# Loading the first four row tiles of x in two column halves, one on each hardware DMA queue

## The chip, the cores and the metric

The kernel runs on one core of a Trainium2 chip. The metric is the device time of one execution in microseconds (us), and lower is better. Most executions of one kernel lie within 0.3% of each other.

## The reference

```python
# x (16, 512, 768), w1 (768, 3072), b1 (3072), w2 (3072, 768), all float32
y = np.matmul(x, w1) + b1
y = np.maximum(y, 0)
return np.matmul(y, w2).astype(np.float32)
```

Seen as one matrix, x has 8192 rows of 768 numbers. One row is 3072 bytes.

## The kernel before

The kernel multiplies in fp16 and uses a scheme that needs fewer block products than the plain one. TensorE is the bound for nearly the whole run. What matters here is its opening, the first 20 us.

The first 512 rows of x are fetched as four row tiles of 128 rows, in fp32, on the two hardware queues, which SyncE (`nc.sync`) and ScalarE (`nc.scalar`) issue: tiles 0 and 2 on the first, 1 and 3 on the second. Each partition of a tile takes one whole row.

```python
def load_x_first(self):
    self.first_rows = []
    for s in range(4):
        o = self.o_pool.tile([P, 2, self.NH], FP32, name="o")     # NH = 384
        o = o.rearrange("p a n -> p (a n)")
        (self.nc.sync, self.nc.scalar)[s % 2].dma_start(
            out=o, in_=self.xf[s * P:(s + 1) * P, :])
        self.first_rows.append(o)

def bias(self):                                                    # cut
    nc.scalar.dma_start(out=self.b1_rows, in_=self.b1.rearrange("(t p) -> t p", p=P))
```

The weights w1 come in strips, each of two transfers that GpSimd issues on its software queue and that turn fp32 into fp16 on the way. The next 512 rows of x (tile `xn`) take the same way.

```python
def load_strip(self, w, c, t):                                     # cut
    for half in range(2):
        self.nc.gpsimd.dma_start(out=w[:, 2 * half:2 * half + 2]..., in_=w1r[:, :, h0:h0 + P])

def run(self):                                                     # cut: the opening
    self.load_x_first()
    self.bias()
    self.load_w1(0)
    self.constants()              # GpSimd and VectorE: identity, ones, bounds
    self.load_w1(1)
    self.load_w1(2)
    self.load_x(0, (1,), 2)       # xn, in two parts
    self.load_w1(3)
    ...                           # w2 and more
    self.warm()                   # 8 matmuls of ones (x16 instructions in the trace)
    self.transpose_x_first(0)
```

TensorE first runs some matmuls of ones while it waits for x, then transposes the four tiles, six blocks of 128 x 128 each. VectorE copies the first three blocks out of PSUM, ScalarE the other three:

```python
def transpose_x_first(self, half, which=range(4)):
    for s in which:
        rows = self.raw[1][:, s, :] if half else self.first_rows[s]
        for a in range(2):
            ...
            for k in range(3):
                nc.tensor.transpose(ps[:, k, :],
                                    rows[:, (3 * a + k) * P:(3 * a + k + 1) * P], ident)
            o = self.x[:, 2 * half + a, :, s * P:(s + 1) * P]
            if a:
                nc.scalar.copy(out=o, in_=ps)
            else:
                nc.vector.tensor_copy(out=o, in_=ps)
```

Only when all four are done do the first products with w1 begin (line 563 of the kernel, in parts of 256 columns, then line 544 in full width). A few groups later the transposes of `xn` follow.

## Time and profile before

| what | before |
|---|---|
| median of three runs | 874.22 us (874.20 to 874.57) |
| span of the profiled run | 872.9 us |
| TensorE busy | 864.6 us |
| row tiles 0 to 3 of x landed, on the last engine | 5.18, 5.40, 7.01, 7.31 us |
| first packet of the software queue | 6.15 us |
| first product with w1 begins | 8.42 us |
| two parts of xn landed | 16.13, 18.08 us |

The landings are the times at which the last of the 16 DMA engines had added to the transfer's semaphore. How to read the rest: TensorE is idle for 8 us in 873, and nearly all of that lies at the two ends. The views of this kernel that the argument rests on stand in the prediction below. One view more will be needed, the timeline of TensorE over the first 9 us (start, length, line and operation, count, and in brackets the idle time ahead of it with its releaser):

```profile
5.32 1.50 PE L493 MATMUL ps<-ident,o 128*128 128x128 f32 x12 [0.38 <-DMA o<-in_x_dram]
7.05 1.53 PE L493 MATMUL ps<-ident,o 128*128 128x128 f32 x12 [0.23 <-DMA o<-in_x_dram]
8.42 0.82 PE L563 MATMUL ps<-x,w1s 128*128 128x256 f16 x6
```

The transposes come in two bursts, two tiles each, since the four loads land in two pairs.

### The profile page before, as it was taken

What the parts mean: (1) busy time and instruction counts of PE and PEld (TensorE: products, weight loads), DVE (VectorE), ACT (ScalarE), POOL (GpSimd) and SP (SyncE); (2) the same over time, 40 slices, a digit from 0 to 9 for tenths busy, and PEclk for the clock granted to TensorE, in tenths of its full rate; (3) what the DMA queues carried; (4) which work ended last, traced back from release to release, by engine and by line L of the source; (5) the groups of instructions that cost most, each with busy time, mean ns of one, the idle gap of its engine ahead of it and who ended that gap; (6) DMA issues with size and microseconds to landing.
All of it is one profiled execution on the core that took longest, in us unless ns stands there. A gap on an engine that the chain in (4) does not pass through costs nothing.

```text
span 872.9 us, 12620 instructions
## 1 busy us (share of the span) xinstructions
PE 864.6 (99%) x4693; PEld 458.8 (53%) x4693; DVE 621.4 (71%) x1082; ACT 521.3 (60%) x789; POOL 198.5 (23%) x175
## 2 busy tenths in 40 slices
PE   9999999999999999999999999999999999999997
PEld 7454554545545454554545546455454555545454
DVE  3898767767686667866799776666866758666676
ACT  5765667866677766676355776766626345263450
POOL 6310240603305041040200402203031130401325
PEclk9999999999999999999999999999999999999999
DMA  9999598796979959549551836539174482736724
GB/s 205 199 230 263 111 275 209 133 266 129 292 160 188 272 79 279 127 175 346 219 186 55 129 97 169 95 130 141 56 143 74 145 127 108 111 54 161 111 73 146
DMA packets 122532, 141.24 MB, mean 162 GB/s; under 512 B 67276, under 2 KB 115940, under 8 KB 118628
## 3 DMA queue, kind: packets, MB, share of 16 engines
q0 software_dynamic: 48512, 43.26, 35.0%
q1 hardware_dynamic: 73216, 95.76, 33.8%
q10 hardware_dynamic: 740, 1.39, 0.4%
q8 instruction: 37, 0.61, 0.3%
q14 instruction: 27, 0.22, 0.1%
HBM read 75.31 MB, written 77.66 MB: 175 GB/s over the span
## 4 chain that ended last, share of the span: by engine, by line
PE 97%; DMA 1%; POOL 1%; issue 0%; DVE 0%; POOLq 0%
PE ps L705 48%; PE ps L606 47%; PE ps L544 2%; DMA xn<-in_x_dram 1%; POOL w1s L332 1%; PE ps L563 0%; PE ps L493 0%; DVE o L738 0%; POOL ident masks.py:199 0%; POOL ident L285 0%; POOL high L300 0%; POOL low L301 0%; POOL ident masks.py:197 0%; PE ps L788 0%; PE ps L798 0%
## 5 line engine op out<-in xcount | busy, mean ns | idle before, releaser
L705 PE MATMUL ps<-v,y 128*128 128x384 f16 x2560 | 423.8, 326 | 0.0
L606 PE MATMUL ps<-x,w1s 128*128 128x512 f16 x1890 | 415.9, 379 | 0.0
L705 PEld LDWEIGHTS <-y 128*128 128x128 f16 x2560 | 249.3, 98 | 171.9 <-ACT y L623 2.7
L606 PEld LDWEIGHTS <-w1s 128*128 128x128 f16 x1890 | 184.7, 98 | 218.2 <-issue 1.0
L526 DVE TENSOR_TENSOR y<-y 128x512 f16<-128x512 f16 x512 | 204.6, 426 | 31.5 <-ACT y L623 24.1
L614 ACT ACTIVATE s<-ps,b1y 128x512 f32<-128x512 f32 x210 | 142.1, 686 | 136.1 <-PE ps L606 55.6
L618 DVE CUSTOM_DVE_ANT_0 y<-ps,s 128x512 f16<-128x512 f32 x210 | 144.9, 690 | 102.6 <-PE ps L606 71.3
L744 ACT ACTIVATE s<-ps 128x768 f32<-128x768 f32 x94 | 76.0, 809 | 112.7 <-PE ps L705 91.3
L763 POOL DMA_DIRECT2D out_dram<-o x54 | 66.4, 1375 | 315.9 <-DVE o L750 315.9
L750 DVE TENSOR_TENSOR s<-ps,s 128x768 f32<-128x768 f32 x96 | 90.2, 953 | 13.5 <-ACT s L744 6.7
L623 ACT ACTIVATE y<-ps,b1y 128x512 f16<-128x512 f32 x90 | 61.8, 687 | 37.5 <-PE ps L606 37.5
L750 DVE TENSOR_TENSOR o<-s,ps 128x768 f32<-128x768 f32 x53 | 50.4, 952 | 46.8 <-PE ps L705 23.2
L750 DVE TENSOR_TENSOR o<-ps,s 128x768 f32<-128x768 f32 x55 | 51.4, 953 | 31.8 <-ACT s L744 30.7
L452 POOL TENSOR_TENSOR x<-x 128x3072 f16<-128x3072 f16 x7 | 42.1, 6018 | 55.2 <-DVE x L449 43.5
L332 POOL DMA_DIRECT2D x<-in_w_dram x12 | 10.1, 848 | 183.8 <-PE ps L606 121.6
L440 ACT ACTIVATE scrap<-xn 128x768 f16<-128x768 f16 x60 | 50.4, 840 | 1.2
L629 ACT ACTIVATE ps<-ps,b1y 128x512 f32<-128x512 f32 x60 | 39.5, 659 | 10.3 <-PE ps L606 7.6
L744 ACT ACTIVATE ps<-ps 128x768 f32<-128x768 f32 x32 | 25.4, 795 | 17.9 <-PE ps L705 17.9
L623 ACT ACTIVATE y<-ps 128x512 f16<-128x512 f32 x60 | 35.8, 597 | 0.2
L401 ACT ACTIVATE scrap<-scrap 128x1536 f16<-128x1536 f16 x24 | 35.5, 1479 | 0.4
L427 POOL DMA_DIRECT2D xn<-in_x_dram x16 | 12.1, 759 | 69.4 <-ACT scrap L440 68.3
L544 PE MATMUL ps<-x,w1s 128*128 128x512 f16 x114 | 24.9, 379 | 0.0
(74 smaller groups left out, 303.3 us busy)
## 6 DMA issues: line engine op xcount, KB each, us to landing
out_dram<-o SPq DMA_DIRECT2D x54, 384.0 KB, 5.5
out_dram<-o POOLq DMA_DIRECT2D x54, 384.0 KB, 6.0
xd<-x SPq DMA_DIRECT2D x8, 1536.0 KB, 5.6
x<-xd SPq DMA_DIRECT2D x8, 1536.0 KB, 8.2
xn<-in_x_dram POOLq DMA_DIRECT2D x14, 768.0 KB, 9.3
xd<-x SPq DMA_DIRECT2D x7, 1152.0 KB, 9.6
x<-xd SPq DMA_DIRECT2D x7, 1152.0 KB, 5.3
out_dram<-x SPq DMA_DIRECT2D x16, 384.0 KB, 7.0
```

Of the source, the lines that this page charges most:

```text
L440: self.nc.scalar.activation(out=self.junk(self.K), in_=rows, func=ACTF.Square, accum_out=self.stat[:, i:i + 1])
L452: (self.nc.gpsimd if it > 1 else self.nc.vector).tensor_tensor(out=x[:, a21:self.XS2 + 1:self.XS2 - a21], in0=x[:, a21:self.XS1 + 1:self.X ...
L526: self.nc.vector.tensor_tensor(out=pair(*outs), in0=pair(*ins0), in1=pair(*ins1), op=ALU.add if sign > 0 else ALU.subtract)
L544: nc.tensor.matmul(ps, lhsT=w[:, ws[i], k, :], rhs=x[:, xs[i], k, :], start=(i == 0 and k == 0), stop=(i == 1 and k == 2))
L606: nc.tensor.matmul(ps, lhsT=w[:, slot, k, :], rhs=x[:, xslot, k, :], start=(start and k == 0), stop=(k == 2), skip_group_check=True)
L614: nc.scalar.activation(out=kept(name), in_=ps, func=ACTF.Identity, bias=bias)
L618: nc.vector._custom_dve(TENSOR_ADD_SAT, out=self.y_of(self.TP * half + t, m), in0=self.two(ps), in1=self.two(kept(name)), s0=F_MAX, s1=0.0)
L623: nc.scalar.activation(out=self.y_of(self.TP * half + t, m), in_=self.two(ps), func=ACTF.Relu, **kw)
L705: nc.tensor.matmul(self.ps[:, 2 * q + j, 0:NH], lhsT=self.y[:, U_OF[p], m0:m0 + P], rhs=self.v[:, V_OF[p], s, :], start=(start and s == 0) ...
L744: nc.scalar.activation(out=o, in_=ps, func=ACTF.Copy, scale=float(sign))
L750: nc.vector.tensor_tensor(out=o, in0=a, in1=b, op=ALU.add if sign == kept_sign else ALU.subtract)
L763: nc.gpsimd.dma_start(out=rows, in_=o, accum_op=ALU.add)
```

## The change

The intent: with both queues working on the same tile, tile 0 should be complete earlier than when each queue works on a tile of its own, and TensorE, which waits for x, could begin earlier. Each row of 3072 bytes is fetched as two pieces of 1536.

```diff
         for s in range(4):
             o = self.o_pool.tile([P, 2, self.NH], FP32, name="o")
-            o = o.rearrange("p a n -> p (a n)")
-            (self.nc.sync, self.nc.scalar)[s % 2].dma_start(
-                out=o, in_=self.xf[s * P:(s + 1) * P, :])
-            self.first_rows.append(o)
+            for a, queue in enumerate((self.nc.sync, self.nc.scalar)):
+                queue.dma_start(out=o[:, a], in_=self.xf[s * P:(s + 1) * P,
+                                                         a * self.NH:(a + 1) * self.NH])
+            self.first_rows.append(o.rearrange("p a n -> p (a n)"))
```

## The prediction

> **What bounds the kernel now.** I read the page first, for which engine is the bound and where its few idle microseconds lie; then TensorE's list of waits; then the chain of waits over the first 22 us, since the change touches nothing later; then the DMA queues in stretches, because the chain ends on a transfer there. The page: TensorE is busy 864.6 of 872.9 us, the mean granted clock is 0.999, and the slices show full digits everywhere.
>
> ```profile
> PE   9999999999999999999999999999999999999997
> ...
> PE 97%; DMA 1%; POOL 1%; issue 0%; DVE 0%; POOLq 0%
> ```
>
> The reader is to see that there is no slack on TensorE after the first slice: whatever the opening loses or wins moves the end by the same amount, and nothing but the opening can be won by a change of the first loads. TensorE's waits, all of the run, add up to 2.1 us (waits under about 0.1 us are not in the list):
>
> ```profile
> PE ps L415 <- DVE ones L294: 1.3, 1, 1.3
> PE ps L493 <- DMA o<-in_x_dram: 0.6, 2, 0.4
> PE ps L493 <- DMA xn<-in_x_dram: 0.2, 1, 0.2
> ```
>
> The second line is the one that the change aims at: the transposes of the first four row tiles (tile o) wait 0.6 us for x. It looks as if 0.6 us could be won. The chain of waits over the first 22 us (start, length, what) says otherwise:
>
> ```profile
> 8.01 8.11 DMA xn<-in_x_dram
> 16.13 0.05 issue
> 16.17 0.84 PE ps L493 x12
> 17.02 1.31 PE ps L563 x12
> 18.33 0.79 PE ps L493 x12
> ```
>
> The chain doesn't pass through tile o at all. It passes through xn, the second 512 rows of x, which GpSimd loads as fp16 in two parts: TensorE starts the transposes of the first part at 16.17, just after its landing at 16.13. The second part, issued at about 8.7 us, took 9.4 us to land, so it landed at about 18.1 us, and TensorE begins the transposes of it then, with hardly a gap (the modelled end of the matmul before is 18.32). So TensorE is pinned to a DMA landing twice, at 16.1 and at 18.1 us, and everything it does before can only be early for that.
>
> Why do these transfers take 8 to 9 us? The DMA queues, 0 to 6 us and then 7 to 18 us:
>
> ```profile
> q1 hardware_dynamic: 255, 0.73, 34.9%
> q10 hardware_dynamic: 216, 0.61, 27.6%
> ```
> ```profile
> q0 software_dynamic: 5668, 2.07, 158.0%
> q10 hardware_dynamic: 1, 0.00, 0.0%
> ```
>
> Until 6 us only the two hardware queues moved packets, although GpSimd issued its first w1 strips at 1.53 and 2.54 us. From 7 us on only the software queue moves, its packets taking 158% of the 16 engines' time (over 100%, since packets on one engine overlap). So the DMA engines are one serial resource from 2 us to beyond 18 us: x first (until about 6.8 us), then six w1 strips, then xn. The landing of xn is the end of that line, and what matters of x is **when its last byte has left the engines**, not when its first tile lands.
>
> **What the Trainium skill says.** All from the page "DMA: Bandwidth & Descriptors". (1) Section "Issuing engines are not separate DMA queues": DMAs of any issuing engine run on the same 16 DMA engines and interleave. The trace agrees as to the shared engines. (2) Section "Queues, rings and completion order": each engine goes round the queue rows that have work, at packet granularity. Here the trace does not look like it: no software packet in the first 6 us, though its issues are 3 us old. I can't tell from this trace whether the software descriptors were late or held back. (3) Section "Why small descriptors are slow (HBM only)": a fixed cost of about 3 cycles per packet at 32 bytes per cycle. For 3072 bytes this is 96+3 cycles, for twice 1536 bytes 2 x (48+3) = 102, so 3% more as an estimate from that page; the measured rates below show less. (4) Section "Why a DMA increments its semaphore by 16 and not by 1": use one semaphore per transfer in flight. This matters here, because the changed kernel has nine hardware transfers at the start where its semaphores are eight.
>
> **The change part by part.**
>
> Removed: four loads of 128 x 3072 bytes, two per queue. Added: eight of 128 x 1536 bytes, four per queue. Bytes the same, 1.57 MB; packets 512 become 1024.
>
> (a) Time on the DMA engines. Two stretches give the rate by packet size; the first holds 3072-byte reads of x (3 to 6 us), the second 1536-byte reads of earlier output (793 to 795.5 us):
>
> ```profile
> DMA packets 421, 1.20 MB, mean 398 GB/s; under 512 B 32, under 2 KB 32, under 8 KB 421
> ```
> ```profile
> DMA packets 682, 0.99 MB, mean 398 GB/s; under 512 B 35, under 2 KB 682, under 8 KB 682
> ```
>
> Without the semaphore packets (those under 512 B): 389 packets in 3 us over 16 engines are 123.4 ns per packet and engine; 647 in 2.5 us are 61.8 ns. So x needs 512/16 x 123.4 = 3.95 us before, and 1024/16 x 61.8 = 3.96 us after. The load of x ends where it did, the software queue starts where it did, and xn lands where it did: **0.0 us**, with 0.1 us (the page's 3%) as the size of what I may have missed.
>
> (b) The order of landings. Before, tiles 0 and 1 share the engines half and half and land at about 5.2 and 5.5 us (TensorE's first transpose starts at 5.32), tiles 2 and 3 at about 7.0 and 7.3. After, both queues work on tile 0, then on 1, 2, 3. Spread evenly over the same stretch these land at about 4.4, 5.3, 6.3 and 7.3 us. The first transpose can then start when the warm-up matmuls end (1.29 + 3.65 = 4.94 us), 0.4 us earlier. Tile 3, the last, lands as before; its six transposes (0.76 us, half of the 1.53 us for twelve) end at 8.1 to 8.2 instead of 8.58. So the wait of 0.6 us nearly goes, and the transposes end 0.4 us earlier.
>
> (c) What TensorE does with it. The next matmul (line 563) needs the first w1 strip: issued at 1.53 us, landed 6.8 us later, that is at 8.33; its weight load starts at 8.36. So that wait takes the place of the one removed, and about 0.0 to 0.1 us of the 0.4 is left. Were it all kept, there are still the landings of xn: TensorE had only 0.16 us to spare at 16.17.
>
> (d) The extra issues. Each costs its queue some 0.41 us (two took 0.91 us on ScalarE's, 0.87 on SyncE's), so ScalarE spends 0.8 us more. Besides, the built order of instructions shows a new wait: with eight semaphores for hardware transfers, the ninth, the bias load on ScalarE's queue, now waits for one half of tile 0 to land, about 4.4 us. ScalarE's activation table load stands behind it:
>
> ```profile
> 1.91 0.65 ACTq L309 DMA_DIRECT2D b_rows<-in_b_dram  x1
> 2.59 1.28 ACT L497 ACT_TABLE_LOAD   x1 [2.59 <-issue]
> ...
> 6.20 0.48 ACT L497 CAST x<-ps 128x384 f16<-128x384 f32 x1 [2.32 <-PE ps L493]
> ```
>
> So after: 4.4 + 0.65 + 1.28 = 6.3 us, against a first copy at 6.20 us before. The four copies of 0.48 us follow the transposes; the last, of tile 3, would end at about 8.7 (before 8.62 + 0.48 = 9.1). Even if the half landed at 5.2 us, four copies from 7.1 us end at 9.1, no later than before. The bias itself is transposed at 9.17 us; issued at 4.4 to 5.1 it stands in the queue behind the same halves of x as before, and 12 KB should land by 7.5 us. This **costs nothing**, if tile 0 isn't late.
>
> (e) All later hardware transfers move on by four of eight semaphores: a permutation, each still waits for the one eight before it.
>
> Sum on the path that sets the end: 0.0 (a), -0.1 to 0.0 (c), 0.0 (d). I put 874.3 us, the time of before and a tenth for the packets.
>
> **The rivals.** First, the wait for o is real and 0.4 us are won: 873.8. For it speaks the list of waits; against it the w1 strip at 8.33 and xn at 16.13 and 18.1. Second, twice the packets make the load of x longer, because the opening isn't in the steady state: between 2 and 4 us the engines were 84% busy and the rate was 267 GB/s, not 398. If half-sized packets fill the start worse, by up to 0.5 us, all the software line moves with it and TensorE too: 874.7. Third, the software queue gets more turns beside smaller packets: w1 earlier, tile 3 later, the sum of work the same and xn where it was: 874.2. Fourth, the bias or table load becomes the wait: only if tile 0 landed after about 6 us, against (b); then 0.3 to 0.5 us more. None reaches 1% of the time.
>
> **Range and chances.** The three runs before lie 0.37 us apart, as much as any effect here. With rivals of -0.4 to +0.5 us and this scatter, I take 873.7 to 875.0. A change of 2% would be 17.5 us, some thirty times the 0.6 us of wait; 98% for the same, 1% each side for an accident.
>
> **What would show it.** In the changed profile: first transpose at about 4.95 us and the wait on o under 0.3 us (b); a new short idle of TensorE or its weight load at about 8.2 to 8.4 us, put down to w1 or to issue (c); the table load at about 5.0 us (d); the software queue's first packets still after 6 us, and xn still landing at 16.1 and 18.1 us, within 0.2 (a). The prediction is wrong if the landings of xn move by more than 0.5 us, or if TensorE has a gap after 22 us that it hadn't.

## The result, and the profile after

| | before | after |
|---|---|---|
| median of six runs | 874.48 us (874.20 to 874.57) | 875.78 us (875.29 to 876.50) |
| span of the profiled run | 872.9 us | 873.9 us |

The ratio of after to before is 1.0016, with a 95% interval of 1.0003 to 1.0029. A ratio here is the mean time of one kernel's runs over that of the other's in the same rounds, so it is not quite the ratio of the medians. The result is correct and within 2%, as predicted, but it is 0.8 us above the top of the predicted range, and slower by more than the scatter. A repetition on another chip (the run e18 below) gave 875.98 against 874.43, ratio 1.0016 again.

The page of the changed kernel, its TensorE slices and the chain that ended last:

```profile
PE   8999999999999999999999999999999999999997
...
PE 98%; DMA 1%; issue 0%; SPq 0%; DVE 0%
```

The first slice has fallen from 9 to 8 and nothing else has changed: the time came from the opening. TensorE's wait for x (total us, number, longest):

```profile
PE ps L493 <- DMA o<-in_x_dram: 2.6, 2, 1.6
```

The wait for tile o, which the change aimed at, was 0.6 us and is now 2.6 us. The waits for xn have gone from the list. The chain of waits over the first 22 us (start, length, what) passes elsewhere than before:

```profile
2.37 7.23 DMA o<-in_x_dram
9.60 0.14 issue
9.74 0.85 PE ps L493 x6
```

It now runs through the half of tile 3 that was issued at 2.37 us and landed 7.2 us later, and no longer through xn. On TensorE's timeline:

```profile
4.52 1.57 PE L493 MATMUL ps<-ident,o 128*128 128x128 f32 x12
7.68 1.01 PE L493 MATMUL ps<-ident,o 128*128 128x128 f32 x6 [1.59 <-DMA o<-in_x_dram]
9.74 0.85 PE L493 MATMUL ps<-ident,o 128*128 128x128 f32 x6 [1.05 <-DMA o<-in_x_dram]
10.42 0.82 PE L563 MATMUL ps<-x,w1s 128*128 128x256 f16 x6
```

The reader is to see both faces of the change. The first two tiles did come earlier: their transposes start at 4.52 us instead of 5.32, with no wait at all. But tiles 2 and 3 were complete 1.1 and 2.5 us later (8.09 and 9.77 us), and as the products begin only after the fourth tile, the first of them starts at 10.42 us instead of 8.42.

The products need the first strip of w1 too. The weight load with which they begin, before and after:

```profile
8.36 0.59 PEld L563 LDWEIGHTS <-w1s 128*128 128x128 f16 x6
10.34 0.62 PEld L563 LDWEIGHTS <-w1s 128*128 128x128 f16 x6
```

The strip was complete at 8.31 us before, and at 10.29 after (10.18 in the repetition e18), both times just ahead of this line. So two late loads hold the first product at the same place: tile 3, whose last transposes run until 10.58, and the strip. With x on time alone it could not have begun before 10.3 us.

Here is how the 2.0 us travel to the end. The first full-width product (line 544 after the transposes of xn) starts at 22.85 instead of 21.00, 1.85 us later; the last group of 144 matmuls of line 705 on the chain at 843.55 instead of 841.97, 1.58 later; the span is 1.0 us longer in this pair of profiled runs, and 1.3 us in the medians. So the kernel gives back some 0.4 us of the 2.0 on the way. The last store is issued at 868.89 instead of 867.32, 1.57 later (1.47 in e18). What follows that store took 5.6 us before and 5.0 after, and anything from 4.1 to 5.8 us in the traces. This end scatters by more than the whole effect, so the last store is the better mark to compare two traces by.

Why did tile 3 land late? The DMA queues of the changed kernel over 0 to 6 us (packets, MB, share of the 16 engines' time) answer to those that the prediction shows for before:

```profile
q1 hardware_dynamic: 422, 0.58, 33.4%
q10 hardware_dynamic: 400, 0.55, 27.9%
q0 software_dynamic: 160, 0.04, 6.8%
```

Before, the two hardware queues had moved 0.73 + 0.61 = 1.34 MB by 6 us; now 0.58 + 0.55 = 1.13 MB, and the software queue is there already. Over 6 to 9.5 us, first before, then after:

```profile
q0 software_dynamic: 1998, 0.50, 145.3%
q10 hardware_dynamic: 108, 0.18, 14.3%
```
```profile
q0 software_dynamic: 1192, 0.30, 87.3%
q10 hardware_dynamic: 205, 0.25, 24.2%
q1 hardware_dynamic: 154, 0.21, 21.6%
```

In the changed kernel x and the software queue share the engines for all this stretch. My own count of the records of single packets, by the microsecond of their start, shows it more finely: KB of x (with the 12 KB of the bias), then packets of w1.

```text
us            2     3     4     5      6      7      8      9
before  KB  150   372   387   408    231      0      0      0
        w1    0     0     0     0    255    702     ..     ..
after   KB  216   336   342   207    160    165    112      8
        w1    0     0     0   160    278    180    415    611
```

Two things differ. From 3 to 5 us, with x alone on the engines in both kernels, the changed one moves 678 KB where the other moves 759; but from 2 to 3 us it had moved more, so that by 5 us the two are nearly level, at 894 and 909 KB. And the first software packet comes at 5.13 us instead of 6.15, with 606 KB of x still to move instead of 153. From then on x gets 110 to 210 KB per us where it had 400. Its last packet ends at 9.26 instead of 6.88 us. In this pair, then, nearly all of the difference comes after the software queue's early start. The stretches from 4 to 5 and 5 to 6 us (window, then the busy share of PE, PEld, DVE, ACT and POOL, the granted clock, the share of the DMA engines and GB/s) show the same, before and after:

```profile
4.00:5.00 1.00, 0.94 (x6) 0.75 (x4) 0.00 (x0) 0.00 (x0) 0.96 (x10) 1.00 1.03 396
5.00:6.00 1.00, 0.68 (x7) 0.71 (x7) 0.13 (x1) 0.00 (x0) 1.00 (x2) 1.00 1.03 418
```
```profile
4.00:5.00 1.00, 1.00 (x11) 1.00 (x10) 0.00 (x0) 0.14 (x1) 0.96 (x10) 1.00 0.97 350
5.00:6.00 1.00, 1.00 (x10) 0.73 (x7) 0.76 (x2) 1.00 (x1) 1.00 (x2) 1.00 1.21 253
```

From 396 and 418 GB/s to 350 and 253. Note that the DMA share is hardly lower, and in the second stretch higher: a share counts how long packets were under way, not how much they carried.

### The profile page after: what moved, and what is told of

Read it like the earlier page. It is cut to its first block, busy times and chain, and to the rows that moved or that the text cites. A ratio compares the mean times of both kernels' runs of the same rounds, so it can differ in the third digit from the quotient of the medians.

```text
span 873.9 us, 12627 instructions
## 1 busy us (share of the span) xinstructions
PE 864.3 (99%) x4693; PEld 459.2 (53%) x4693; DVE 621.5 (71%) x1082; ACT 521.1 (60%) x789; POOL 198.5 (23%) x175
## 4 chain that ended last, share of the span: by engine, by line
PE 98%; DMA 1%; issue 0%; SPq 0%; DVE 0%
PE ps L705 47%; PE ps L606 47%; PE ps L544 3%; DMA o<-in_x_dram 1%; PE ps L563 1%; PE ps L493 0%; SPq L478 0%; DVE o L738 0%; PE ps L315 0%; PE ps L788 0%; PE ps L798 0%; DVE o L750 0%
## 5 line engine op out<-in xcount | busy, mean ns | idle before, releaser
L623 ACT ACTIVATE y<-ps,b1y 128x512 f16<-128x512 f32 x90 | 61.8, 687 | 37.5 <-PE ps L606 37.5
L332 POOL DMA_DIRECT2D x<-in_w_dram x12 | 10.1, 848 | 184.3 <-PE ps L705 63.2
L629 ACT ACTIVATE ps<-ps,b1y 128x512 f32<-128x512 f32 x60 | 39.5, 659 | 10.3 <-PE ps L606 7.6
```

The lines of the kernel that those rows point to most:

```text
L623: nc.scalar.activation(out=self.y_of(self.TP * half + t, m), in_=self.two(ps), func=ACTF.Relu, **kw)
```

## The experiments

My theory after this comparison had two parts: pieces of 1536 bytes use the engines worse while x is alone on them, and the software queue then gets in while much of x is outstanding and takes turns with it. The rivals are named in the expectations, at some places by a letter: **W**, it is the bias load's wait for a half of tile 0, or the number of transfers against eight semaphores; the order of the halves over the queues; **P**, the engines handle only so many packets per time; **H**, it matters which tiles are split, not how many; **G**, each transfer needs some 0.5 us of preparation; **Q**, trouble comes after a fixed number of packets; **R**, it takes two queues with small packets. Eighteen runs were made, all with a correct result. In the text "x done" is the end of the landing of its last piece, and "the first product" the start of line 563 on TensorE (its number shifts a little with the edit).

### Halves by rows (e1)

```diff
+            for a, queue in enumerate((self.nc.sync, self.nc.scalar)):
+                r = slice(a * 64, a * 64 + 64)
+                queue.dma_start(out=o[r], in_=self.xf[s * P:(s + 1) * P, :][r])
```

Eight transfers as in the change, but with whole rows of 3072 bytes, 64 partitions each.

> Each of the first four row tiles is split by rows (64 partitions on each hardware queue) instead of by k: eight transfers and nine hardware transfers with the bias as in the change, both queues on one tile, but packets of 3072 bytes, 512 in all, as before the change. Theory A (small packets: with packets of 1536 bytes the software queue gets in before x is through and takes engine time from it): the first software packet at 6 us or later, the last tile landed by 7.5 us, 874.2 to 874.8 us. Rival B (number of transfers, the ninth on eight semaphores, or both queues on one tile): software packets from about 5.1 us, last tile landed at 9 us or later, 875.3 to 876.5 us as in the change.

Measured: 879.18 us (877.84 to 880.51) against 874.50, ratio 1.0059 [1.0042, 1.0075]; x done at 10.77 us, the first product at 11.99, the first software packet at 4.50 with 987 KB of x left. This is worse than the change. A packet of 3072 bytes took 155 ns in the median here, and 204 between 4 and 5 us, where it takes 121 ns in the kernel before. So the run is confounded: a transfer to 64 partitions is another thing than one to 128, and it can't tell how the number of transfers acts. It shows only that large packets alone don't make eight transfers harmless.

### Both halves on the tile's own queue (e2)

```diff
+            queue = (self.nc.sync, self.nc.scalar)[s % 2]
+            for a in range(2):
+                queue.dma_start(out=o[:, a], in_=...)     # as in the change
```

> The halves of k are kept, but both halves of a tile go on the tile's own queue as before the change (tiles 0 and 2 SyncE, 1 and 3 ScalarE). Same packets, same number of transfers per queue as in the change; only the order over the queues is the old one. Theory A (small packets): software packets from about 5.1 us, the last half landed at 9 us or later, 875.3 to 876.5 us. Rival C (both queues on one tile at a time): as the kernel before, last half landed by 7.5 us, 874.2 to 874.8 us.

Measured: 875.95 us (875.02 to 878.33), ratio 1.0013 [0.9996, 1.0030]; x done at 9.88, the first product at 11.55, the first software packet at 5.55 with 451 KB left. x is as late as in the change although tiles 0 and 1 are again loaded side by side. The order of the halves over the queues is not the cause of that. (The time alone would not show a loss, as the interval includes 1; and the trace is that of the slowest of the four runs, 878.33 us, with the clock at half from 10.4 to 13.7 us.)

### The software queue kept away from x (e3, e5)

```diff
-        self.load_w1(0)
         self.constants()
+        gate = self.const.tile([P, 2], FP32, name="gate")
+        for s in range(4):
+            self.nc.gpsimd.tensor_copy(out=gate, in_=self.first_rows[s][:, 0:self.K:self.NH])
+        self.load_w1(0)
```

GpSimd reads two columns of each tile before it issues w1, so x has the engines to itself. e3 is this on top of the change, e5 on top of the kernel before.

> The change, with the software queue kept empty until x has landed: GpSimd makes the constants first, then reads two columns of each of the four tiles, and only then issues the first w1 strip. Theory A (contention with the software queue): x alone lands by 7.4 us, as the prediction had it, in the order 4.4, 5.3, 6.3, 7.3. Rival D (two queues of half-sized packets are not supplied fast enough, whatever else runs): the last half lands at 8 us or later even so. In both the software line starts later than in the change, at about 9.5 us instead of 5.1, and the time is longer, about 877.5 to 878.5 us.

> The same gate on the kernel before the change: the pair of e3. x lands at 7.0 to 7.4 us as without the gate. Theory A: time within 0.3 us of e3 (877.5 to 878.5 us), since without contention the split costs nothing. Rival D: e3 is longer than this by 0.7 us or more.

Measured: e3 880.36 us, ratio 1.0064 [1.0047, 1.0081]; e5 879.90, ratio 1.0061 [1.0044, 1.0077]. Both are slow, as w1 comes late, and some 2 us slower than I had expected: after TensorE's long wait of 3 to 4 us its clock stayed at half for a while. The stretches tell the two apart. The stretches of e5 from 5 to 7 us, then of e3 (same columns as above):

```profile
5.00:6.00 1.00, 0.55 (x4) 0.50 (x4) 0.00 (x0) 0.00 (x0) 0.37 (x2) 1.00 1.02 415
6.00:7.00 1.00, 1.00 (x6) 1.00 (x6) 0.56 (x1) 0.00 (x0) 0.00 (x0) 1.00 0.61 234
```
```profile
5.00:6.00 1.00, 1.00 (x6) 1.00 (x6) 0.18 (x1) 0.82 (x1) 0.27 (x2) 1.00 0.89 315
6.00:7.00 1.00, 1.00 (x7) 1.00 (x7) 0.38 (x1) 0.94 (x2) 0.01 (x1) 1.00 0.88 320
```

With nothing else on the engines, whole rows move at 415 GB/s until they are through at 6.80 us; the halves at some 320, and they are through at 8.02. This is the cleanest pair: the split by itself costs x **1.2 us** on otherwise empty engines. Each is one trace, but five gated looks below agree in sign: from first packet to last, x took 4.79 us in e5, 6.00 in e3, and 5.1 to 6.6 in e11, e14, e17, e20 and e22, all with smaller packets than e5.

What the software queue adds is less certain. In the changed kernel x is through at 9.26 us (8.82 in e18), 1.2 (0.8) us after e3, where whole rows lose 0.1 by it (6.88 - 6.80). But the pair of e10 and e14 below, with packets of the same size, is through at 8.60 us with the software queue and at 8.64 without. So the cost of small packets alone is shown. That x moves more slowly once the software queue is in is shown too, by the KB above; how much later x ends for it, these runs don't settle, and the two costs can't simply be added.

### Small packets without more transfers (e10)

```diff
-            o = self.o_pool.tile([P, 2, self.NH], FP32, name="o")
-            o = o.rearrange("p a n -> p (a n)")
+            o = self.s.rearrange("p b n -> p (b n)")[:, s * 784:(s + 1) * 784]
+            o = o.rearrange("p (a n) -> p a n", a=2)[:, :, 0:self.NH]
             (self.nc.sync, self.nc.scalar)[s % 2].dma_start(
-                out=o, in_=self.xf[s * P:(s + 1) * P, :])
+                out=o, in_=self.xf[s * P:(s + 1) * P, :].rearrange("p (a n) -> p a n", a=2))
```

The four transfers of the kernel before, but into a buffer with a gap in the middle of each row, so that each is made of 256 packets of 1536 bytes. There are no more than eight transfers, so the bias load waits for nothing.

> The kernel before with its four transfers of x, but into a buffer with a gap between the halves of a row, so that each transfer consists of 256 packets of 1536 bytes: the change's packets (1024 in all) with the old number of transfers (four, no bias wait). Theory P (the packet count: more, smaller packets on the hardware queues let engines run out of hardware packets, and the software queue steps in early): first software packet at 5.0 to 5.7 us, last tile landed at 9 us or later, 875.0 to 876.5 us. Rival T (the number of transfers, each with its end on every engine): as the kernel before, first software packet at 6 us or later, last tile landed by 7.5 us, 874.2 to 874.8 us.

Measured: 876.25 us (875.88 to 877.02) against 874.29, ratio 1.0024 [1.0008, 1.0041]; x done at 8.95, the first product at 11.27, the first software packet at 5.40 with 597 KB left. x is nearly as late as in the changed kernel (9.77 us, and 9.25 in e18), without the change's transfers: it is **the packets**, and neither the number of transfers nor the bias load's wait. Two things are in the way of a finer reading. The first packet of x came at 2.42 us here, 0.4 later than before. And TensorE ran its transposes at half clock:

```profile
8.99 2.44 PE L496 MATMUL ps<-ident,s 128*128 128x128 f32 x12 [0.43 <-DMA s<-in_x_dram]
```

Twelve transposes took 1.53 us in the kernel before. So some 0.9 of the 2.5 us by which the last store is late in this trace (869.82 us) is the clock's, and not that of a late x.

### Which tiles are split (e6, e9, e4, e16, e19)

```diff
+            if s in (0,):          # e6; (0, 1) in e9, (1, 2, 3) in e4, (2, 3) in e16 and e19
+                ...                # two halves, as in the change
+            else:
+                ...                # whole, as before
```

> Only tile 0 is split over both queues, tiles 1 to 3 whole as before: five transfers of x and the bias, no wait on a semaphore before the bias. Both theories P and T: a quarter of the change, so most of x lands as before (last tile by 7.6 us) and the time is 874.3 to 874.9 us. If the dry engines come from any split at all: last tile at 9 us or later, 875.3 us or more. First transposes start at 4.95 us.

> Tiles 0 and 1 are split, 2 and 3 whole: half of the change (768 packets, six transfers of x). P and T: between, first software packet at 5.3 to 6.2 us, last tile landed at 7.3 to 8.5 us, 874.4 to 875.3 us.

> Tiles 1 to 3 are split, tile 0 is whole: seven transfers of x, so the bias is the eighth and does not wait for a landing; the activation table is loaded at about 3 us again. Rival W (the new wait of the bias and of the table load matters): 874.2 to 874.8 us as the kernel before. P and T: nearly the whole of the change, last tile landed at 8.5 us or later, 875.0 to 876.3 us.

> Tiles 2 and 3 are split, 0 and 1 whole: as many packets and transfers as e9, which split 0 and 1 and took 877.2 us, in the other order. Theory H (the feed must build up a lead with large packets before small ones come; a split at the start takes that lead away): last tile landed by 8.3 us, 874.2 to 875.0 us. Rival (only the number of small packets counts): as e9, last tile at 9 us or later, 875.6 to 878 us.

| run | split | us (n = 4) | ratio, 95% interval | first software packet (KB of x left) | x done | first product |
|---|---|---|---|---|---|---|
| e6 | 0 | 874.58 | 1.0005 [0.9989, 1.0022] | 5.92 (195) | 7.76 | 9.12 |
| e9 | 0, 1 | 877.21 | 1.0033 [1.0016, 1.0049] | 6.11 (420) | 9.18 | 11.25 |
| e4 | 1, 2, 3 | 874.63 | 1.0003 [0.9987, 1.0020] | 5.99 (313) | 8.45 | 9.27 |
| e16 | 2, 3 | 873.51 | 0.9993 [0.9976, 1.0009] | 6.00 (252) | 7.45 | 8.39 |

e4 alone looked like rival W: with three of four tiles split, but no wait of the bias load, the loss nearly vanishes. e9 and e10 contradict that, since they have no such wait either and lose. What tells them apart is where the small packets stand: e9 and e16 both split two tiles, so that they have the same number of transfers and packets, and x is done 1.7 us apart. The stretch from 4 to 5 us of e9 and of e16:

```profile
4.00:5.00 1.00, 1.00 (x7) 1.00 (x6) 0.00 (x0) 0.36 (x1) 0.95 (x10) 1.00 0.81 267
```
```profile
4.00:5.00 1.00, 0.75 (x6) 0.56 (x4) 0.00 (x0) 0.35 (x1) 0.96 (x10) 1.00 0.97 364
```

In e9 the engines are not full (0.81) from 4 us on, two microseconds before the first software packet. **Small packets hurt when they come first**, and cost next to nothing behind two tiles of whole rows (rival H was right). That the times of e4 and e6 lie within the scatter of before fits with their first product, 0.7 to 0.85 us later than 8.42, of which some is taken up again at xn.

I ran e16 a second time, with the change itself beside it, as its first result looked like a gain:

> e16 (tiles 2 and 3 split, 0 and 1 whole) beside e18 on one chip. Theory H (the first tiles must go whole, so that the feed gets ahead of the engines): last tile landed by 8 us, 873.2 to 874.6 us, less than e18 by 1 us or more. Rival (e16 was luck): 875 us or more.

> The changed kernel unaltered, for a second trace of its landings and as the partner of e19 on one chip. Software packets from 5.1 to 5.8 us, the last half of tile 3 landed at 9 to 10 us, 875.0 to 876.5 us.

Measured: e19 875.07 us (873.63 to 875.81), ratio 1.0012 [0.9995, 1.0028]; e18 875.98 (875.09 to 876.23), ratio 1.0016 [0.9999, 1.0033]. The landings repeat well: in e19 x is done at 7.59 and the first product starts at 8.40, in e18 at 9.25 and 10.22. The times of e16 and e19 don't agree with each other by 1.6 us, and their mean is that of before. In their two traces the last store is issued at the same 867.43 us, 0.11 after that of before; the difference lies behind it. So splitting tiles 2 and 3 is not shown to be faster or slower than before, and no version beats it.

### Why e9 lost more than the whole change (e15)

e9 splits half of what the change splits and loses 2.9 us against 1.3. TensorE's timeline of e9 around its gap:

```profile
9.03 2.43 PE L499 MATMUL ps<-ident,o 128*128 128x128 f32 x12 [2.09 <-DMA o<-in_x_dram]
11.25 1.49 PE L569 MATMUL ps<-x,w1s 128*128 128x256 f16 x6
```

After one wait of 2.09 us twelve transposes take 2.43 us instead of 1.5, and six products 1.49 instead of 0.82: TensorE ran at half clock, from 9.5 to 12.9 us (single transposes at 421 ns instead of 273). In the changed kernel the wait is broken into 1.59 and 1.05 us, and the clock stayed up. So I filled the gap:

```diff
+            for _ in range(8 if s == 2 and not half else 0):
+                nc.tensor.matmul(self.ps[:, 5, 0:P], lhsT=self.ones, rhs=self.ones, start=True,
+                                 stop=True)
```

> e9 (tiles 0 and 1 split) with eight matmuls of the warm-up kind between the transposes of tiles 1 and 2, where TensorE waited 2.1 us in e9 and then ran at half the clock (421 ns instead of 273 ns per matmul) until about 13 us. Theory K (the clock drop after the wait adds about 1.5 us): no half clock, 875.3 to 876.2 us, with the landings of e9. Rival (the late landing of x alone makes e9's time): 876.5 us or more, as e9.

```profile
9.32 1.53 PE L502 MATMUL ps<-ident,o 128*128 128x128 f32 x12 [0.33 <-DMA o<-in_x_dram]
10.69 0.82 PE L572 MATMUL ps<-x,w1s 128*128 128x256 f16 x6
```

Measured: 874.86 us (874.50 to 874.89) against 874.08, ratio 1.0009 [0.9992, 1.0025], somewhat better than expected. x is as late as in e9 (9.46 us), the clock stays full, and some 2 us of time have gone. The last store, 3.15 us later than before in e9, is 1.84 later here. The clock made most of e9's loss in time; it has no part in the change's, where the clock is 1.00 from 8 to 14 us. (e1, e2 and e23 have the same 3.4 us of half clock in their traces, so their times and first products hold more than a late x. "x done" does not depend on it.)

### Small packets alone on the engines: what kind of limit? (e11, e14, e17)

These and the next two are with the gate of e3, to see how x moves by itself. e11: as e10, with six pieces of 512 bytes per row. e14: e10 with the gate. e17: each tile in four quarters of columns, 16 transfers of 768-byte pieces on alternating queues.

```diff
+            for a in range(4):                                     # e17
+                cols = slice(a * 192, a * 192 + 192)
+                (self.nc.sync, self.nc.scalar)[a % 2].dma_start(
+                    out=o[:, cols], in_=self.xf[s * P:(s + 1) * P, cols])
```

> Measures the feed of the two hardware queues by packet count, with nothing else running: the kernel before, gated as e5, with each of the four transfers of x cut into 768 packets of 512 bytes (3072 in all). The software queue moved 512-byte reads at 22.9 ns per engine in the runs before (350 packets in 0.5 us), so the engines themselves could move 3072 of them in about 4.4 us. Theory P as a limit of feed (packets of the hardware queues come one every 4 ns or slower, whatever their size): x takes 12 us or more, from 2 to 14 us or later. Rival (the feed isn't limited by count, only unevenly shared): x is through by 7.5 us. The total is only a by-product: longer by some 2 us in the rival's case, by 8 us or more in P's.

> e10 (four transfers, 1024 packets of 1536 bytes) gated as e3 and e5, so x runs alone. In e3 (eight transfers of the same packets) its last packet ended at 8.02 us, in e5 (512 packets of 3072 bytes) at 6.80. Theory P (packet count): about 7.5 to 8.3 us here. Rival T (transfers): 6.8 to 7.1 us.

> What limits the feed: x in sixteen transfers of 128 packets of 768 bytes, gated, so that x runs alone. The first eight go out without a wait; each needs only some 0.26 us of the engines (8 packets of about 32 ns on each). Theory G (preparing a hardware transfer of 128 rows costs about 0.5 us, one transfer after another over both queues, so that with halves of k the feed just keeps pace with the engines and never gets ahead): the first landings of the first eight transfers come 0.45 to 0.6 us apart and the engines are busy 50 to 65% between 2.5 and 5 us. Rival (transfers are prepared faster; the dry engines have another cause): 0.25 to 0.35 us apart, busy 90% or more until the first eight are through.

Measured: e11 881.05 us, e14 880.22, e17 882.18 (against 874.1 to 874.4 of before). In e11 x needs from 2.43 to 8.20 us, 5.8 us for 3072 packets; in e14 from 2.42 to 8.64, 6.2 us for 1024 packets. Three times the packets in less time: a limit on packets per time (P) is out. In e17 the first six transfers land at 3.02, 3.20, 3.48, 3.76, 4.06 and 4.32 us on their first engine, 0.2 to 0.3 us apart, with the engines 88% busy or more; a preparation of 0.5 us for each (G) is out too. What e14 and e17 share is something else: from the third transfer (e14) or the fifth (e17) on, single engines fall behind. In e14 the third transfer was complete on the first engine at 5.91 and on the last at 8.04. From 7.4 to 8.6 us the engines were 7% busy, which is one of sixteen, with the last 20 packets of x. The records don't name a packet's engine; but 15 packets were in flight on average from 4.5 to 6.1 us, where it had been 17, so that an engine pausing there, which e20 takes for granted, is likely and not shown. In e17 the fifth transfer landed from 4.06 to 5.66.

In all kernels I looked for the same sign in single packets. I counted those that took over 250 ns and started after 4.5 us (a packet of 1536 bytes takes 65 ns, one of 3072 bytes 121):

```text
before 0   e5 0   e16 0   e19 0   e4 0   e6 4   after 10   e18 1   e2 2   e9 12   e15 11
e10 5   e3 2   e14 3   e22 6   e20 7   e11 0   e17 4   e23 7   e1 25
```

The five kernels whose first tile comes in whole rows of 128 partitions (before, e5, e16, e19, e4) have none; of the others all but e11 have some, up to 1151 ns long (after). But the count doesn't go with the loss: e6, without one, has four, more than e18 and e2. So this sign is not the whole of the matter.

### Later, or on one queue (e20, e22, e23)

```diff
+            self.nc.gpsimd.memset(o[:, 0, 0:1], 0.0)          # e20: e14, x issued later
+            self.nc.sync.dma_start(...)                       # e22: e14, all four on SyncE
+            self.nc.sync.dma_start(out=o[:, a], ...)          # e23: the change, all on SyncE
```

> e14 (x alone, four transfers of 256 packets of 1536 bytes) with x issued later, behind GpSimd's constants, by some 1.5 us. In e14 the third and fourth transfers landed unevenly (2.1 us between their first and last engine) because an engine paused from about 4.5 to 6.1 us. Theory Q (the pause comes after so many packets of the hardware queues): it moves with the issue, to 6 us or later, and the third and fourth transfers again spread by 1.5 us or more. Rival (something else at 4.3 to 6 us of the clock disturbs an engine): the pause stays at 4.5 to 6 us, in the first two transfers, and the last two spread by 1 us or less.

> e14 with all four transfers on SyncE's queue. Theory R (two queues taking turns make engines run dry, since the packets of the one are prepared behind those of the other): with one queue no pause, landings spread by 0.8 us or less, x through by 7.3 us. Rival Q (so many small packets, however queued): spread of 1.5 us or more in the last transfers, x through at 8 us or later.

> The change with all eight halves on SyncE's queue (ScalarE's has only the bias), software queue ungated. Theory R: last tile landed by 8 us, 874.0 to 874.9 us. Rival Q: as the change, 9 us or later and 875.2 us or more.

Measured: e20 881.94 us (single look). x moves from 3.90 to 8.97, in 5.07 us where e14 took 6.2, and the transfers' first and last engines lie 0.7 to 0.9 us apart, so that no engine falls far behind. So the lag comes neither after a fixed number of packets (Q) nor at a fixed time. e22 881.64 (single look): x through at 8.56, and the last two transfers are 1.54 and 1.41 us apart between the engines, so that one queue has the trouble too. e23: 878.73 us (876.74 to 879.35) against 874.68, ratio 1.0041 [1.0024, 1.0058]; the first software packet comes at 3.95 with 1090 KB left, x is done at about 11.4, the first product starts at 12.22. R is out, by e22. e23 adds little to that, since SyncE alone issues the eighth half only at 4.27 us (2.39 in the change). It fits the second part of the theory: the software queue gets in at 3.95, 5.13 and 6.15 us in e23, the change and before, and the earlier it does, the later x is done; the late issues may have their part in it.

**What stays open** is why single engines fall behind when the first tiles come in small pieces, and why starting 1.5 us later (e20) lessens it. The runs show when it happens and what it costs, not what an engine waits for. Open, too, are how much of the loss is the software queue's, and what lets it in: room on the engines alone doesn't, since in e9 they were 0.81 and 0.83 full from 4 to 6 us and its first packet came only at 6.11.

## Why the prediction was wrong, and where it was right

**Step (a) failed**: "The load of x ends where it did, the software queue starts where it did, and xn lands where it did: 0.0 us". The two rates that it divides by do hold where packets flow, as packets of 65 and 121 ns show. But they come from the middle of a flow (3 to 6 us) and from near the end of the run (793 us), and the load of x is all opening. There, halves cost x 1.2 us without any neighbour (e3 against e5). And the software queue, which I had taken to follow x, came in the middle of it: first packet at 5.13 us instead of "still after 6 us", with 606 KB of x outstanding instead of 153. x was through at 9.26 us instead of 6.88. xn landed at 17.69 and 19.57, 1.56 and 1.5 us later. By the prediction's own test, "The prediction is wrong if the landings of xn move by more than 0.5 us", it was wrong.

**Step (b) half held.** The first transposes were to start at 4.94 us and started at 4.52. That tile 0 would be there in time was right; the rest was luck, as the matmuls of ones took 3.38 us in this trace (3.43 in e18) and 3.65 in that of before. In e2 and e9 they took nearly 3.8, and the transposes began at 4.87. But "Tile 3, the last, lands as before" failed with (a): 9.77 instead of 7.31 us (9.25 in e18), and its transposes ended at about 10.6 and not 8.2. (Tile 1 of the kernel before, read as 5.5 us, landed at 5.40; nothing hangs on it.)

**Step (c) failed in consequence.** The w1 strip that was to land at 8.33 us landed at 10.29, as it shared the engines with x, and TensorE was without tile 3 about as long. And xn, the pin on which the prediction hung the whole opening, let go: TensorE came to its first part at 17.85, after it had landed, and waited for neither. The opening was pinned by the strip and then by xn before, and is pinned by tile 3 and the strip now. The 2.0 us are therefore not a shift of xn by 1.5 us, although the two are of one origin and nearly of one size.

**Step (d) held.** The bias load waited as read from the order of instructions, the table load ran at 4.86 us (predicted 5.0) and the first copy of ScalarE at 6.15 (predicted 6.3); nobody waited for them, and e10 shows that the loss is there without this wait. **Step (e) held**: no gap after 22 us.

**The rivals** had named the cause. The second, "half-sized packets fill the start worse", was sized "by up to 0.5 us" from the 84% of busy engines between 2 and 4 us, and measured 1.2 in e3 against e5. The third, "the software queue gets more turns beside smaller packets: w1 earlier, tile 3 later", was right in the turns and in tile 3, and wrong in w1: of the first strip one engine was done earlier (6.83 instead of 7.87 us), but the last 2.0 us later. It was given "the sum of work the same and xn where it was", hence no loss. What I failed to do was to let both happen together, and to ask how much of x would be outstanding if the software queue came in a microsecond earlier: up to 5 us both kernels had moved about the same, and it met four times as much. The range was cut for either of the two in its small form.

**In time**: 2.0 us at the first product, 1.85 at 23 us, 1.58 at 843 us, 1.57 at the last store, 1.3 in the median. This part, that TensorE has no slack and most of an opening's loss arrives at the end, was read rightly.

## What to carry to other kernels

A rate measured in mid-flow did not hold in the opening of this kernel: read it there, and look at the landing of the last piece on the last engine, not of the first, for every transfer that the next step needs (here tile 3 and the first strip of w1). When other transfers stand ready behind an urgent load, give the urgent one large packets first, since whatever of it is still outstanding when the others come in moves more slowly from then on; if it must be cut small, cut its last part (e16), not its first (e9). And a wait in the list is not the gain to be had: here 0.6 us of it stood before a chain that ran elsewhere, and the attempt on it made it 2.6.

## What the Trainium skill lacked or had wrong

- Page "DMA: Bandwidth & Descriptors", section "Why small descriptors are slow (HBM only)": its fixed cost per packet gave an estimate of 3% for 1536 against 3072 bytes. In mid-flow this trace shows even less (2 x 61.8 against 123.4 ns), but in the opening as a whole x in halves took 1.2 us more, through at 8.02 instead of 6.80 us with nothing else on the engines (e3, e5). The section has nothing on an opening.
- Same page, section "Queues, rings and completion order": it lets an engine go round all rows that have work, packet by packet. It gives no figure for how long a row of the software queue can be without packets while other rows have them. In e3 and e5 its first packet came 1.7 us after the issue (9.26 to 10.98, 8.09 to 9.83 us); with x on the engines it took from 1.53 us to 6.15 in the kernel before, to 5.13 after and to 3.95 in e23. It is not a matter of engines with room alone (e9: 0.81 full, and 6.11 us); these runs don't show what holds it, and the page doesn't say.
- Page "TensorE: Matmul & The Clock Gate", Part 1: it lets the clock fall after at least one idle window of about 3.4 us. Here it fell after less: in e9 one wait of 2.09 us was enough for transposes of 421 instead of 273 ns, in e2 one of 1.89, and in e23 the clock was at half from 10.1 us without a wait of more than 0.92. Waits of 1.59 and 1.05 us in the changed kernel, and one of 1.86 in e14, left it up. The runs give no threshold.
- On no page that I found: single DMA engines can fall more than a microsecond behind the others (7.4 to 8.6 us in e14, with 7% of the engines' time busy), so that a transfer's first and last engine finish up to 2.4 us apart (in the changed kernel; 0.4 to 0.5 us in the kernel before). And transfers that lie ready on two queues follow each other every 0.2 to 0.3 us (e17, pieces of 768 bytes).
